# 368 instead of 384 columns in the dense U products of a PEER block: 16 inputs get their U vectors by gather during the gate build

## The chip, the cores and the metric

One core of one Trainium2 chip runs the whole program. The metric is the device time of one execution in microseconds (us); the kernel before takes 1673.26 us (median of 3 runs, 1672.77 to 1673.74). The engines are called as in the profile: PE (TensorE, matrix products), DVE (VectorE), ACT (ScalarE), POOL (GpSimd; it issues the indirect gathers), SP (SyncE; it issues most transfers).

## The reference, cut to what matters

The reference is one decoder layer for 512 inputs ("tokens") of width 1024. The change lies in its second half, a mixer of 16384 experts:

```
q = x @ w_query                                   # 8 heads, 2 halves of 128
s = q . sub_keys                                  # 128 scores for each half
16 best of each half -> 256 sums -> 16 best       # expert number e = i * 128 + j, gate g = softmax
act = gelu(u_table[e] . x)                        # 8 * 16 = 128 experts for each input
out = sum over the 128 experts of g * act * v_table[e]
```

The last lines of the layer are out_layer = layer_norm(ALPHA * x + out). Nothing is approximated in the kernel; float32 products are made of three products of split operands (high*high, high*low, low*high).

## The kernel before, in words

The 512 inputs are split in two. Inputs 384 to 511 (block 3) are served by **gathering**: for each of their 128 expert slots one row of u_table per input is fetched by an indirect DMA and multiplied on DVE, then the same with v_table (`gather`, L1259 on). Inputs 0 to 383 are served **densely**: all 16384 experts are computed for them, in 128 chunks of 128 experts. For chunk c, `u_chunk` (L1108) makes 8 * 3 = 24 products of 384 columns (L68 to L70, called from L1114) into one PSUM tile, and ACT writes the gelu of it to a tile "act" (L1116). Later `v_chunk` (L1249) multiplies that tile by the gates of the chunk (P, L1214), splits it into high and low parts (Ph L1227, Pl L1234) and makes 18 products of 512 columns with the chunk of v_table, which add to six PSUM tiles (`va`, L1243 to L1247). So a pair of one U chunk and one V chunk is 24 + 18 products.

The gates of the dense inputs must be there as a dense array: for every chunk of 128 experts and every input a gate or zero. `build_g` (L1025) makes it in 48 **groups** of 8 inputs. For a group, `hot` (L1028) compares the two halves of each expert number with an iota (two comparisons, oj L1036 and oi L1037) and multiplies one of the results by the high and low part of the gate (g L1038, oi L1039), all float16 on DVE; PE multiplies them (16 products of 128 columns, L1055 and L1056); ACT copies PSUM to a staging tile (L1058); after every fourth group SP stores that tile to DRAM (`gsp`, L1062). The V chunks read it back (`gt`, L1202): the first read needs all 12 stores, and the first P needs the first read.

Weights: every item (a chunk of u_table or v_table, 512 KB) goes through a stream: SP loads it to one of 3 raw tiles, ACT rounds it to the high part (wih, L105), DVE subtracts for the low part (wil, L115). The low part of item n + 2 is issued when item n is taken, and there are 3 tiles for it, so it waits until PE is done with item n - 1.

**The order of the work.** Each engine works strictly in program order, and the program is written by a planner at build time. Before the V chunks can start, 54 U chunks (LEAD, L1187) and the gates must be done. The planner (`drive`, L1154) keeps two sums: tm[0] is the time that it has given to PE (T_U = 4.24 for a U chunk, 1.1 for a group), tm[1] is that of DVE (2.7 for a group, 1.2 for the split of an item). Whenever tm[0] <= tm[1] and fewer than 54 U chunks have been written, it writes a U chunk, otherwise the next piece of DVE's work: routing (`stage1` L940, `stage2` L955), then the groups. What is left of the 54 U chunks is written after the last group (L1187). Then come the V chunks, each behind a U chunk until there are 128; the gather of block 3 is mixed into them at an even pace (L1338 to L1343).

The last part (`ln_out`, L1362) adds ALPHA * x to the sums, normalises and stores; for block 2 this is the end of the program.

Of the kernel before, what the change touches and what calls it, by code (L numbers as in the profile page):

```python
# [24 lines left out]
D = 1024  # L25
NB = 4
# [3 lines left out]
SCALE = 192.0 ** -0.5  # L30
NT = 384
LEAD = 54
LASTC = 120
T_U = 4.24
T_Q = 6.3
# [14 lines left out]
def tile_block(ctx: ExitStack, tc: tile.TileContext, I, out):  # L50
# [139 lines left out]
    gsp = dram.tile([NT // 32, 128, 128, 32], F32, name="gsp")  # L190
    acd = dram.tile([64, 128], F32, name="acd")

    wst = pool("wst")
# [662 lines left out]
    XTH = xt.tile([128, 8, S], F32R, name="XTH")  # L856
    XTL = xt.tile([128, 8, S], F32R, name="XTL")
    lnq = pool("lnq", side="right")
    ROW = lnq.tile([128, 2, D], F32, name="ROW")
# [95 lines left out]
    def stage2():  # L955
# [38 lines left out]
        sh = [128, 16, 16, 16]  # L994
        for b in range(NB):
            eq = rt2.tile([128, 16, 16, 16], F16, name="eq")
            abv = abf[:, b].rearrange("p e (h k) -> p (e h) k", k=16)
            V.tensor_tensor(eq, abv[:, :, None, :].to_broadcast(sh), iaE[:, None].to_broadcast(sh), op=OP.is_equal)
            yield 2.3
            eqv = eq.rearrange("p g a (k c) -> p (g a) k c", c=2)  # L1000
            tv = ti[:, b].rearrange("p e h a c -> p (e h a) c")
            V.tensor_tensor(eqv, eqv, tv[:, :, None, :].to_broadcast([128, 256, 8, 2]), op=OP.mult)
            yield 2.3
            for w in (8, 4, 2):
                V.tensor_tensor(eq[:, :, :w], eq[:, :, :w], eq[:, :, w:2 * w], op=OP.add)
# [5 lines left out]
    GT = {}  # L1011

    def g_head(b):
        ijg = IJG.pop(b)
        ps = px()
        for e in range(3):
            T.transpose(ps[:, e * 128:(e + 1) * 128], ijg[:, e].rearrange("p h k -> p (h k)"), ident)
        ijT = ijp.tile([128, 2, 128], F16, name="ijT", bufs=2)
        gT = ijp.tile([128, 2, 128], F16, name="gT", bufs=2)
        A.activation(ijT.rearrange("p a b -> p (a b)"), ps[:, 0:256], AF.Copy)  # L1020
        A.activation(gT[:, 0], ps[:, 256:384], AF.Copy, scale=GSC)
        V.scalar_tensor_tensor(gT[:, 1], ps[:, 256:384], GSC, gT[:, 0], op0=OP.mult, op1=OP.subtract)
        GT[b] = ijT, gT

    def build_g():  # L1025
        bc = [128, 4, 128, 2]

        def hot(n):  # L1028
            ijT, gT = GT[n // 16]
            t0 = n % 16 * 8  # L1030
            col = lambda z: z[:, t0:t0 + 8].rearrange("p (q c) -> p q c", c=2)[:, :, None, :].to_broadcast(bc)
            oj = gb.tile(bc, F16, name="oj", bufs=2)
            oi = gb.tile(bc, F16, name="oi", bufs=2)
            g1 = gb.tile(bc, F16, name="g1", bufs=2)
            io = iotaE[:, None].to_broadcast(bc)
            V.tensor_tensor(oj, io, col(ijT[:, 1]), op=OP.is_equal)  # L1036
            V.tensor_tensor(oi, io, col(ijT[:, 0]), op=OP.is_equal)  # L1037
            V.tensor_tensor(g1, oi, col(gT[:, 1]), op=OP.mult)  # L1038
            V.tensor_tensor(oi, oi, col(gT[:, 0]), op=OP.mult)  # L1039
            return oj, oi, g1  # L1040

        nxt = hot(0)
        yield 2.7
        for n in range(48):
# [18 lines left out]
            if g == 12 and b < 2:  # L1063
                g_head(b + 1)
            yield 2.7 if n < 47 else 0.1

# [37 lines left out]
    win.ha = 1  # L1104
    ap_ = pool("act")
# [71 lines left out]
    drive(fill)  # L1177
    close(rq)
    rt2 = pool("rt2")
    lo_on[0] = V  # L1180
    drive(stage2())
    close(rt2)
    close(rt)
    gb = pool("gb", side="right")
    drive(build_g())
    uc = un[0]
# [33 lines left out]
    def v_sb(c, nm):  # L1220
        if c > LASTC:
            return ap_.tile([128, NT], F32, name="act", bufs=LEAD).bitcast(F32R)
        return vst.tile([128, NT], F32R, name=nm, bufs=3)
# [138 lines left out]
    def ln_out(b):  # L1362
# [4 lines left out]
        for e in range(2):  # L1367
            V.scalar_tensor_tensor(t[:, ce[e]], t[:, ce[e]], ALPHA, va[b][e], op0=OP.mult, op1=OP.add)
            yield
# [13 lines left out]
        for e in range(2):  # L1383
# [102 lines left out]
```

## Time and profile before

| | |
|---|---|
| median of 3 runs | 1673.26 us |
| the profiled execution | 1676.3 us |
| its span, first to last instruction | 1674.3 us |
| PE / DVE / ACT / POOL busy | 97% / 81% / 41% / 27% |
| routing and gates, beside U chunks 2 to 53 | 540 to 829 us |
| first group of the gates / end of the last | 640 / 802.6 us |
| first V product | 829.3 us |
| last U chunk's gelu | 1439.9 us |

The profile shows one execution. Rows of a timeline give the start in us, the duration, the engine, the line of kernel.py, and the tiles (out<-in); in square brackets stands the idle time of the engine before it, and what ended that. In a table of windows each engine has its busy time and number of instructions (x), then the granted clock of TensorE (1.00 is full), the busy share of the DMA engines, and GB/s. "Busy" durations of neighbouring instructions on one engine overlap: the distance from one start to the next is what an instruction costs in a stream.

### The profile page before, as it was taken

The numbers are of one execution on the slowest core, as the hardware profiler recorded it, in microseconds if no ns is written. First come the engines' busy times: TensorE is split into PE (matmuls) and PEld (weight loads), VectorE is DVE, ScalarE is ACT, GpSimd is POOL, SyncE is SP. The second block draws the span as 40 slices with busy tenths as digits, with TensorE's granted clock in tenths as the row PEclk, the third lists the DMA queues.
The fourth block names the chain that finished last, engine by engine and source line by source line (L and its number), as shares of the span: only waits on it lengthen the run. The fifth ranks groups of instructions, "written<-read, shape, count | busy, mean of one in ns | idle before, by whom it ended". The sixth has DMA issues, their size and how long they took to land.

```text
span 1674.3 us, 23581 instructions
## 1 busy us (share of the span) xinstructions
PE 1622.4 (97%) x8639; PEld 1429.5 (85%) x8639; DVE 1363.2 (81%) x2674; ACT 685.0 (41%) x1082; POOL 450.6 (27%) x314
## 2 busy tenths in 40 slices
PE   7999989999999999999999999999999999999997
PEld 5877868888888998999999999999999999888886
DVE  8978688847399999999477878778788888989887
ACT  5573556631333344555433333333333333333331
POOL 0000000000333400000055555545454444653300
PEclk9999999999999999999999999999999999999999
DMA  6342121464432335667699999999999999999973
GB/s 238 102 151 76 45 62 46 111 237 138 124 96 76 101 114 158 244 227 258 203 361 341 330 322 332 330 346 319 321 339 335 333 321 341 341 351 332 339 228 124
DMA packets 146211, 384.80 MB, mean 230 GB/s; under 512 B 11936, under 2 KB 62368, under 8 KB 144304
## 3 DMA queue, kind: packets, MB, share of 16 engines
q1 hardware_dynamic: 105536, 237.24, 42.3%
q0 software_dynamic: 40416, 145.80, 24.3%
q8 instruction: 67, 1.10, 0.3%
q14 instruction: 48, 0.39, 0.1%
q10 hardware_dynamic: 144, 0.26, 0.0%
HBM read 350.72 MB, written 31.49 MB: 228 GB/s over the span
## 4 chain that ended last, share of the span: by engine, by line
PE 75%; DVE 20%; ACT 2%; issue 2%; DMA 1%; SPq 0%; DVEq 0%; ACTq 0%
PE va L1243 10%; PE va L1244 10%; PE va L1247 10%; PE pu L68 8%; PE pu L70 8%; PE pu L69 8%; DVE wil L115 2%; PE pa L69 2%; PE pa L70 2%; PE pa L68 2%; PE pw L69 1%; PE pw L70 1%; PE pw L68 1%; DVE t L931 1%; DVE g L1038 1%
## 5 line engine op out<-in xcount | busy, mean ns | idle before, releaser
L115 DVE TENSOR_TENSOR wil<-wir,wih 128x1024 fp32r<-128x1024 f32 (+1 forms) x250 | 297.4, 1190 | 113.0 <-issue 56.7
L105 ACT ACTIVATE wih<-wir 128x1024 fp32r<-128x1024 f32 (+2 forms) x269 | 277.9, 1034 | 228.5 <-DMA wir<-v 96.7
L70 PE MATMUL pu<-XTH,wil 128*128 128x384 f32 x1008 | 342.7, 340 | 4.7 <-DVE wil L115 4.7
L68 PE MATMUL pu<-XTH,wih 128*128 128x384 f32 x904 | 309.9, 343 | 1.0 <-ACT sc L917 1.0
L69 PE MATMUL pu<-XTL,wih 128*128 128x384 f32 x904 | 307.1, 340 | 0.0
L1280 POOL DMA_INDIRECT row<-u,ix x128 | 188.5, 1473 | 434.5 <-DMA wir<-v 262.1
L1244 PE MATMUL va<-wil,Ph 128*128 128x512 f32 x726 | 283.6, 391 | 0.0
L1280 POOL DMA_INDIRECT row<-v,ix x128 | 185.2, 1446 | 200.4 <-DVE ac L1297 170.8
L70 PEld LDWEIGHTS pu<-XTH,wil 128*128 128x128 f32 x1008 | 190.3, 189 | 5.0 <-DVE wil L115 5.0
L1116 ACT ACTIVATE act<-pu 128x384 f32<-128x384 f32 x126 | 61.9, 491 | 316.4 <-PE pu L70 316.3
L68 PEld LDWEIGHTS pu<-XTH,wih 128*128 128x128 f32 x904 | 170.9, 189 | 4.0 <-ACT sc L917 1.2
L69 PEld LDWEIGHTS pu<-XTL,wih 128*128 128x128 f32 x904 | 170.9, 189 | 2.8
L1243 PE MATMUL va<-wih,Ph 128*128 128x512 f32 x432 | 168.6, 390 | 0.0
L1297 DVE SCALAR_TENSOR_TENSOR ac<-row,hd,ac 128x1024 f32<-128x1024 f32 x128 | 164.0, 1281 | 2.5 <-DMA row<-v,ix 0.3
L1244 PEld LDWEIGHTS va<-wil,Ph 128*128 128x128 f32 x726 | 136.3, 188 | 26.2
L1291 DVE SCALAR_TENSOR_TENSOR row<-row,x 128x1024 f32<-128x1024 f32 x128 | 150.0, 1219 | 1.6 <-DMA row<-u,ix 1.5
L1247 PE MATMUL va<-wih,Pl 128*128 128x512 f32 x432 | 133.3, 390 | 0.0
L105 ACT ACTIVATE wihx<-wir 128x1024 fp32r<-128x1024 f32 x67 | 71.1, 1061 | 143.3 <-DMA wir<-v 88.3
L115 DVE TENSOR_TENSOR wil<-wir,wihx 128x1024 fp32r<-128x1024 f32 x61 | 74.6, 1223 | 63.0 <-issue 57.2
L1243 PE MATMUL va<-wihx,Ph 128*128 128x512 f32 x294 | 115.0, 391 | 1.2 <-ACT Ph L1227 1.2
L115 POOL TENSOR_TENSOR wil<-wir,wih 128x1024 fp32r<-128x1024 f32 x19 | 46.6, 2454 | 190.7 <-PE pw L70 164.2
L1247 PEld LDWEIGHTS va<-wih,Pl 128*128 128x128 f32 x432 | 81.2, 188 | 16.8
(435 smaller groups left out, 3067.7 us busy)
## 6 DMA issues: line engine op xcount, KB each, us to landing
wir<-ut SPq DMA_DIRECT2D x128, 512.0 KB, 5.2
wir<-v SPq DMA_DIRECT2D x128, 512.0 KB, 6.6
gsp<-stg SPq DMA_DIRECT2D x12, 2048.0 KB, 7.3
gt<-gsp SPq DMA_DIRECT2D x32, 768.0 KB, 10.0
wir<-wo SPq DMA_DIRECT2D x26, 512.0 KB, 4.1
wir<-wf SPq DMA_DIRECT2D x18, 512.0 KB, 3.5
wir<-wqr SPq DMA_DIRECT2D x16, 512.0 KB, 3.7
de<-acd POOLq DMA_DIRECT2D x8, 512.0 KB, 5.0
```

Source lines behind the costliest of these rows:

```text
L68: T.matmul(ps, lh, rh, start=start, stop=False)
L69: T.matmul(ps, lh, rl, start=False, stop=False)
L70: T.matmul(ps, ll, rh, start=False, stop=stop)
L105: A.activation(h, r, AF.Copy)
L115: self.lo(n).tensor_tensor(l, r, h, op=OP.subtract)
L1116: A.activation(ACT[c], ps, AF.Gelu)
L1243: T.matmul(va[b][e], Ph[:, bs], h[:, cs], start=c == 0, stop=False)
L1244: T.matmul(va[b][e], Ph[:, bs], l[:, cs], start=False, stop=False)
L1247: T.matmul(va[b][e], Pl[:, bs], h[:, cs], start=False, stop=c == 127)
L1280: G.indirect_dma_start(out=R[s], out_offset=None, in_=I["u"] if s < 128 else I["v"], in_offset=bass.IndirectOffsetOnAxis(ap=ix[:, s % 128: ...
L1291: V.scalar_tensor_tensor(r, r, 1.0, x3, op0=OP.mult, op1=OP.mult, accum_out=hd[:, s:s + 1])
L1297: V.scalar_tensor_tensor(ac, r, hd[:, s - 128:s - 127], ac, op0=OP.mult, op1=OP.add)
```

## The change

The dense U products take 368 columns (NU) instead of 384: the last UG = 16 inputs of block 2 leave them. For these 16 inputs the U vectors are gathered: 16 * 128 rows, taken as 16 indirect DMAs of 128 rows, each multiplied by x and summed on DVE (`ug_dots`), one after every second group from step 2 of the gate build on. Their gelu (128 partitions x 16) goes through DRAM into another layout and is multiplied into the gates of these inputs (`ug_head`, at step 41), scaled by its largest magnitude; the act tiles hold 1.0 in these 16 columns, and `ln_out` of block 2 multiplies the sum by the scale (and takes ALPHA * x from an ACT instruction). The routing treats block 2 first.

The rows and x for these products lie where 8 of the 54 act tiles were, so only 46 (KEEP) U chunks can be written before the last of the 16 products; the 8 others get a pool of their own after it (`act2`, step 34). The planner counts 4.07 for a U chunk, 2.55 for a group, and 1.2 for each gathered product. In `hot` the two comparisons become one instruction of twice the size.

```diff
 NT = 384
+UG = 16
+NU = NT - UG
 LEAD = 54
+KEEP = 46
-T_U = 4.24
+T_U = 4.07
...
-        for b in range(NB):
+        for b in (2, 0, 1, 3):
...
             if b == 2:
+                ug_index(p3)
+            if b == 1:
                 g_head(0)
...
+    def ug_index(tmp):
+        ijg = IJG[2]
+        f = lambda z: z.rearrange("p h k -> p (h k)")
+        ix = tmp[:, :128].bitcast(I32)
+        V.scalar_tensor_tensor(ix, f(ijg[:, 0]), 128.0, f(ijg[:, 1]), op0=OP.mult, op1=OP.add)
+        G.dma_start(ugi, ix[128 - UG:])
+        G.dma_start(ugg, f(ijg[128 - UG:, 2]))
+        G.dma_start(UR["ix"], bass.AP(tensor=ugi.tensor, offset=ugi.offset, ap=[[16, 8], [128, UG], [1, 16]]))
+        G.dma_start(UR["g"], ugg)
+        for n in range(2):
+            ug_fetch(n)
...
+    def ug_dots():
+        for n in range(16):
+            r = UR.pop(n)
+            V.scalar_tensor_tensor(r, r, 1.0, UR["x"], op0=OP.mult, op1=OP.mult, accum_out=UR["hd"][:, n:n + 1])
+            ug_fetch(n + 2)
+            yield 1.2
+        A.activation(UR["hd"], UR["hd"], AF.Gelu)
+        G.dma_start(bass.AP(tensor=ugh.tensor, offset=ugh.offset, ap=[[16, 8], [128, UG], [1, 16]]), UR["hd"])
+        G.dma_start(UR["w"], ugh)
+        close(ug)
+        aps.append(pool("act2"))
+        yield 0.1
+
+    def ug_head():
+        w, g = UR["w"], UR["g"]
+        mx, r = UR["m"][:, 0:1], UR["m"][:, 1:2]
+        V.tensor_tensor(w, w, g, op=OP.mult)
+        V.scalar_tensor_tensor(g, w, -1.0, w, op0=OP.mult, op1=OP.max)
+        V.tensor_reduce(mx, g, axis=AX.X, op=OP.max)
+        V.tensor_scalar(mx, mx, 1.0e-30, None, op0=OP.max)
+        V.reciprocal(r, mx)
+        V.tensor_scalar(w, w, r, None, op0=OP.mult)
+        G.dma_start(scl[128 - UG:], mx)
+        ps = px()
+        T.transpose(ps[:, :UG], w, ident[:UG, :UG])
+        gT = GT[2][1]
+        A.activation(gT[:, 0, 128 - UG:], ps[:, :UG], AF.Copy, scale=GSC)
+        V.scalar_tensor_tensor(gT[:, 1, 128 - UG:], ps[:, :UG], GSC, gT[:, 0, 128 - UG:],
+                               op0=OP.mult, op1=OP.subtract)
...
-            V.tensor_tensor(oj, io, col(ijT[:, 1]), op=OP.is_equal)
-            V.tensor_tensor(oi, io, col(ijT[:, 0]), op=OP.is_equal)
+            V.tensor_tensor(ij.rearrange("p e q i c -> p (e q) i c"), iotaE[:, None].to_broadcast(b2),
+                            ijT[:, n % 16].rearrange("p e (q c) -> p (e q) c", c=2)[:, :, None, :].to_broadcast(b2),
+                            op=OP.is_equal)
+            oi, oj = ij[:, 0], ij[:, 1]
...
-            yield 2.7 if n < 47 else 0.1
+            if n >= 2 and n % 2 == 0:
+                tm[1] += next(dots, 0.0)
+            if n == 41:
+                ug_head()
+                tm[1] += 1.2
+            yield 2.55 if n < 47 else 0.1
...
+    def act_tile():
+        k = an[0] % LEAD >= KEEP
+        an[0] += 1
+        return aps[k].tile([128, NT], F32, name="act", bufs=LEAD - KEEP if k else KEEP)
...
-        ps = (psum or pu)()[:, :NT]
+        ps = (psum or pu)()[:, :NU]
         for k in range(8):
-            mm3(ps, h[:, k], l[:, k], XTH[:, k, :NT], XTL[:, k, :NT], k == 0, k == 7)
-        ACT[c] = ap_.tile([128, NT], F32, name="act", bufs=LEAD)
-        A.activation(ACT[c], ps, AF.Gelu)
+            mm3(ps, h[:, k], l[:, k], XTH[:, k, :NU], XTL[:, k, :NU], k == 0, k == 7)
+        ACT[c] = act_tile()
+        A.activation(ACT[c][:, NU:], one, AF.Copy)
+        A.activation(ACT[c][:, :NU], ps, AF.Gelu)
...
-            if tm[0] <= tm[1] and un[0] < LEAD:
+            if tm[0] <= tm[1] and un[0] < (LEAD if len(aps) > 1 else KEEP):
...
+            if b == 2:
+                V.scalar_tensor_tensor(t[:, ce[e]], va[b][e], scl, t[:, ce[e]], op0=OP.mult, op1=OP.add)
+            else:
+                V.scalar_tensor_tensor(t[:, ce[e]], t[:, ce[e]], ALPHA, va[b][e], op0=OP.mult, op1=OP.add)
...
+    A.activation(xr[2], xr[2], AF.Copy, scale=ALPHA)
```

More of the change, by code (lines that the diff above doesn't have):

```diff
@@ L191, in tile_block @@
     acd = dram.tile([64, 128], F32, name="acd")
+    ugi = dram.tile([UG, 128], I32, name="ugi")
+    ugg = dram.tile([UG, 128], F32, name="ugg")
+    ugh = dram.tile([UG, 128], F32, name="ugh")
     wst = pool("wst")
@@ L857, in tile_block @@
     XTL = xt.tile([128, 8, S], F32R, name="XTL")
+    one = xt.tile([128, UG], F32, name="one")
+    scl = xt.tile([128, 1], F32, name="scl")
+    V.memset(one, 1.0)
+    V.memset(scl, 1.0)
     lnq = pool("lnq", side="right")
@@ L1178, in tile_block @@
     close(rq)
+    ug = pool("ug")
+    UR["x"] = ug.tile([128, D], F32, name="ux")
+    nc.sync.dma_start(UR["x"], bass.AP(tensor=xsp.tensor, offset=xsp.offset + (3 * 128 - UG) * D,
+                                       ap=[[0, 8], [D, UG], [1, D]]))
+    UR["ix"] = ijp.tile([128, 16], I32, name="uix")
+    UR["g"] = ijp.tile([UG, 128], F32, name="ugw")
     rt2 = pool("rt2")
@@ L1184, in tile_block @@
     gb = pool("gb", side="right")
+    UR["hd"] = gb.tile([128, 16], F32, name="uhd")
+    UR["w"] = gb.tile([UG, 128], F32, name="uw")
+    UR["m"] = gb.tile([UG, 2], F32, name="um")
     drive(build_g())
```

26 lines of the change are left out of this document (16 added, 10 removed).

## The prediction

> **What bounds the kernel now.** I read the table of windows first, cut at the borders of the stages: gate build, remaining U chunks, pairs of U and V chunks, V chunks alone, with one narrow window at the start of the pairs. "x" counts instructions; the last two numbers are DMA share and GB/s.
>
> ```profile
> 637.00:803.00 166.00, 157.81 (x1380) 150.48 (x1379) 155.64 (x221) 88.53 (x151) 0.00 (x0) 0.99 0.63 222
> 803.00:829.30 26.30, 25.08 (x143) 24.77 (x141) 5.48 (x6) 8.10 (x12) 0.00 (x0) 1.00 0.76 239
> 829.30:1440.00 610.70, 610.70 (x3068) 556.74 (x3069) 490.92 (x636) 216.49 (x296) 305.53 (x211) 1.00 0.94 330
> 850.00:900.00 50.00, 50.00 (x253) 45.60 (x252) 41.65 (x63) 17.70 (x24) 26.64 (x20) 1.00 0.99 358
> ```
>
> The columns are PE, PEld, DVE, ACT, POOL. From 829 on PE never pauses (610.70 of 610.70): it is the bound there, and a shorter product is a shorter stage. In the gate build it is otherwise: DVE works 155.64 of 166 us, PE 157.81. Both are full, so what is added to DVE there is paid. From 803 to 829 DVE is nearly idle (5.48 of 26.30) while PE works off U chunks. The gelus per stretch count them:
>
> ```profile
> 0.00:638.00 638.00, 14.37 (x26) 0.99 0.36 115
> 638.00:802.40 164.40, 12.28 (x25) 0.99 0.64 225
> 802.40:829.30 26.90, 2.46 (x5) 1.00 0.74 234
> ```
>
> The first count holds two table loads: 24 chunks before the first group, 25 beside the 48 groups, 5 after them. These 5 decide much of what follows, because the first V product must wait for a round trip of the last gates through DRAM. Here are its steps, from the timelines, the transfers and the chain that ended last:
>
> ```profile
> 802.39 0.22 PE L1056 MATMUL pw<-g,oj 128*128 128x128 f16 x1
> 803.30 0.33 SPq L1062 DMA_DIRECT2D gsp<-stg  x1
> gsp<-stg SPq DMA_DIRECT2D x12, 2048.0 KB, 7.3
> 821.71 6.35 DMA gt<-gsp
> 828.13 0.57 DVE P L1214
> 828.73 0.53 ACT Ph L1227
> 829.30 0.50 PE va L1243
> ```
>
> Store issued 0.9 after the last product, 7.3 to land, the read 6.35, P, Ph. Without a queue in between that is 0.9 + 7.3 + 6.4 + 0.1 + 0.6 + 0.6 = 15.9 us. Today it is hidden: 5 U chunks, and chunk 54 behind them, cover 26.9 us.
>
> **The change, part by part.**
>
> *The narrower product.* What counts is the distance of starts, not the duration:
>
> ```profile
> 1000.72 0.34 PE L68 MATMUL pu<-XTH,wih 128*128 128x384 f32 x1
> 1004.96 0.40 PE L1243 MATMUL va<-wih,Ph 128*128 128x512 f32 x1
> 1009.07 0.34 PE L68 MATMUL pu<-XTH,wih 128*128 128x384 f32 x1
> ...
> 217.75 0.28 PE L69 MATMUL pu<-wil,kvh 128*128 128x256 f32 x1
> 218.93 0.28 PE L70 MATMUL pu<-wih,kvl 128*128 128x256 f32 x1
> ```
>
> 24 products of 384 columns take 4.24 us, 0.177 each; the 18 of 512 take 4.11, 0.228 each; ten of 256 take 1.18, 0.118 each. So 16 columns are worth (0.228 - 0.177) / 8 = 6.4 ns by the upper neighbours and (0.177 - 0.118) / 8 = 7.3 ns by the lower; I take 6.9. A U chunk falls by 24 * 6.9 ns = 0.166 us, to 4.07. From V's start on there are 73 chunks on PE's path (55 to 127): **-12.1 us** (bounds -11.3 and -12.8). The stage can take it if the transfers can: they must rise from 330 to about 330 * 8.35 / 8.18 = 337 GB/s, and the narrow window shows 358 with PE at 50 of 50. The first two chunks, before 431 us, give -0.3.
>
> *What DVE gets in the gate build.* A group costs DVE the distance over its four instructions, a split that of L115, a gathered product that of L1291 with its read of the sum:
>
> ```profile
> 798.72 0.68 DVE L1036 TENSOR_TENSOR oj<-iotaE,ijT 128x1024 f16<-128x1024 f16 x1
> 799.32 0.68 DVE L1037 TENSOR_TENSOR oi<-iotaE,ijT 128x1024 f16<-128x1024 f16 x1
> 800.04 0.69 DVE L1038 TENSOR_TENSOR g<-oi,gT 128x1024 f16<-128x1024 f16 x1
> 800.77 0.69 DVE L1039 TENSOR_TENSOR oi<-oi,gT 128x1024 f16<-128x1024 f16 x1
> 801.38 1.22 DVE L115 TENSOR_TENSOR wil<-wir,wihx 128x1024 fp32r<-128x1024 f32 x1
> ...
> 1000.28 1.22 DVE L1291 SCALAR_TENSOR_TENSOR row<-row,x 128x1024 f32<-128x1024 f32 x1
> 1001.43 1.22 DVE L115 TENSOR_TENSOR wil<-wir,wih 128x1024 fp32r<-128x1024 f32 x1
> 1002.57 0.55 DVE L1234 TENSOR_TENSOR Pl<-P,Ph 128x384 fp32r<-128x384 f32 x1
> 834.12 0.28 DVE L1263 SCALAR_TENSOR_TENSOR ix<-ijg 128x128 int32<-128x128 f32 x1
> ```
>
> A group is 801.38 - 798.72 = 2.66 us, a gathered product 1.15, a split 1.14.
>
> - The merged comparison. One instruction of 2048 elements exists in the routing:
>
> ```profile
> L1005 DVE TENSOR_TENSOR eq<-eq 128x2048 f16<-128x2048 f16 x4 | 4.9, 1219 | 0.0
> L1036 DVE TENSOR_TENSOR oj<-iotaE,ijT 128x1024 f16<-128x1024 f16 x48 | 32.9, 686 | 5.0 <-PE pw L1056 4.9
> ```
>
> By durations it saves 2 * 686 - 1219 = 153 ns; by distances only one start, about 0.07 (1024 elements cost 0.60 from start to start, 2048 should cost 1.13). I take distances: 48 * 0.07 = **-3.4** (bounds -7.3 and 0).
> - 16 gathered products: 16 * 1.15 = **+18.4**. Their rows are asked for four groups ahead, over 10 us, so I cost POOL's part at nothing; if that cover fails, each costs a landing.
> - ug_head: seven small DVE instructions like L1263, at 0.28 or a little less, and a transpose and an ACT copy between the last two, on which DVE waits: **+2.4** (bounds 1 and 4). ug_index adds one (0.3); with T_U at 4.07 one more chunk is written before `stage2`, where POOL does the splits (one split less, -1.1): **-0.8** together.
> - Splits that move forward. With the new costs the planner writes U chunks faster: per group tm[1] gains 2.55 + 0.6 and tm[0] 1.1, a chunk closes 4.07 - 1.2 of the gap, so 0.71 chunks a group, where it is (2.7 - 1.1) / (4.24 - 1.2) = 0.53 today (48 groups: 25 chunks, as counted above). All 54 are then written before the last group, 5 more than today: 5 * 1.14 = **+5.7**.
> - The cap. At 0.71 a group the 46th chunk is written at group 28; the pool for the next comes at step 34. In between the gap grows by 6 * 2.05 = 12.3, so four chunks are then written in a row, before group 35's products. What that does to DVE is seen where U chunks run in a row today:
>
> ```profile
> 811.23 1.23 DVE L115 TENSOR_TENSOR wil<-wir,wih 128x1024 fp32r<-128x1024 f32 x1 [3.01 <-PE pu L70]
> 815.47 1.23 DVE L115 TENSOR_TENSOR wil<-wir,wih 128x1024 fp32r<-128x1024 f32 x1 [3.02 <-PE pu L70]
> ```
>
> Each split waits for a low tile until PE is done with an earlier chunk, and everything behind it on DVE, the next comparisons among it, waits too. Four in a row: three distances of 4.07 = 12.2, less 3.4 of splits, less what DVE was ahead, about **+8** (bounds 3 and 9). That is the wait that the change adds; PE is starved in turn from group 28 to 34 and again from 43 on.
>
> Sum: -3.4 + 18.4 + 2.4 - 0.8 + 5.7 + 8 = **+30.3** for the end of the last group, 802.4 -> 832.7. I laid the two engines' queues out instruction by instruction with these durations; for the kernel before this ends at 802.2, for the changed one at 832.7.
>
> *The round trip comes into the open.* No U chunk is left behind the last group but chunk 54 (4.07 us). First V product: 832.7 + 15.9 = 848.6 instead of 829.3, **+19.3** (bounds +7 and +27 from the terms above). PE stands idle some 12 us before it, and an idle PE starts slowly:
>
> ```profile
> 583.38 0.33 PE L69 MATMUL pu<-XTL,wih 128*128 128x384 f32 x1
> 588.43 0.69 PE L70 MATMUL pu<-XTH,wil 128*128 128x384 f32 x1 [4.72 <-DVE wil L115]
> 588.92 0.52 PE L68 MATMUL pu<-XTH,wih 128*128 128x384 f32 x1
> 593.08 0.38 PE L69 MATMUL pu<-XTL,wih 128*128 128x384 f32 x1
> ```
>
> After that pause 13 products take 0.32 apart instead of 0.177: 13 * 0.143 = **+2**.
>
> *At no cost:* the ACT copy of 16 ones per chunk (ACT 216 of 611 us beside the pairs; uncovered it would be a few tenths a chunk), the scaling of x for block 2 (ACT, while PE makes the last products; uncovered about 1 us), ln_out with another operand order (same shape), 8.4 MB of gathered rows in a stretch at 222 GB/s (about 50 more over 166 us, below the 358 shown).
>
> **Sum:** -0.3 + 19.3 + 2 - 12.1 = **+8.9 us**. The terms are of the profiled execution (1676.3 us, span 1674.3), 3.0 above the median of the runs; I add the difference to the median: 1673.26 + 8.9 = 1682.2, in a profiled execution about 1685.2.
>
> **The rivals.**
>
> - *DVE's work is hidden (faster).* If DVE could use its idle time of 803 to 829 before the last group, V's start would be bound by PE's work alone: 52 chunks * 0.166 = -8.6. Then -0.3 - 8.6 - 12.1 = -21, 1652 us. It decides from the point where the gates end before 829.3 - 8.6 - 15.9 = 805, that is at +2 instead of +30. Against it: DVE's 155.64 of 166. Halfway, faster by over 0.2% needs +18 at the gates' end. Chance 0.10.
> - *The catch-up does not stall, and the comparison saves its durations (no change).* 30.3 - 8 - 4 = +18.3 gives +7.3 at V's start, with the pause shorter +1: 7.3 + 1 - 12.4 = -4 to 0; without the one or the other about +1. Around 1672. Chance 0.15.
> - *The pairs do not get shorter (slower still).* Either transfers hold PE (share 0.94 today), or the weight load sets the distance of products. Then 19.3 + 2 = +21, 1694 us. Against it: 358 GB/s with PE full, and 0.118 us at 256 columns with a load for every product; the load is no floor at 0.17. Chance 0.07. By the Trainium skill ("TensorE: Matmul & The Clock Gate", Back-to-back issue gap) a stream of load-and-multiply pairs is spaced about 81 ns at 128 columns and 131 ns at 512, set by both; as an estimate 16 columns would then be worth 2 ns, a chunk 0.05 us, and the whole +17.5. This trace disagrees: 228 ns at 512 columns.
> - *The merged comparison falls to half the rate* through its other access pattern: 48 groups * 1 us more. Chance 0.01.
>
> The rest, 0.67, is the forecast.
>
> **How the numbers follow.** The likeliest is 1682.2. Its own range, from the bounds of its terms (V's start +9 to +26 within most of them, the pairs -11.3 to -12.8), is 1670 to 1690; the range of 8 in 10 reaches part of the way to the third rival and takes in most of the second: 1669 to 1692. A measurement of this kernel can tell about 0.2%, 3.3 us, from no change. Slower by more: most of the forecast and the third and fourth rivals, 0.74; within: 0.14; faster: 0.12.
>
> **What would show it.** In the profile after: U products 0.170 apart; no gelu between groups 29 and 34, then four within 17 us; a DVE wait of several us for PE before the fourth split of those; the last group near 833; the first V product about 16 us behind it, after a PE pause of over 10 us ended by DMA gt<-gsp; pairs of 8.18 us. I am wrong if gelus still stand behind the last group, or if the pairs stay at 8.35.

## The result: 1.0014 times the time before

After the change the kernel takes 1677.12 us (median of 20 runs, 1675.91 to 1678.37), beside 1674.45 us (20 runs) for the kernel before on the same chips: a ratio of **1.0014 [1.0008, 1.0020]**. That is 2.3 us slower by the ratio, where 8.9 us were forecast. The profiled executions say the same: spans of 1676.0 and 1674.3 us, +1.7.

The windows of the kernel after, cut where its stages end (PE, PEld, DVE, ACT, POOL, then granted clock, DMA share, GB/s):

```profile
637.00:833.00 196.00, 172.98 (x1470) 165.55 (x1470) 176.04 (x216) 97.53 (x189) 25.20 (x17) 0.95 0.66 239
833.00:847.00 14.00, 5.73 (x29) 5.42 (x26) 0.56 (x1) 1.27 (x3) 0.00 (x0) 0.74 0.74 253
847.00:1442.00 595.00, 594.87 (x3067) 540.76 (x3068) 491.21 (x635) 223.36 (x371) 304.46 (x211) 0.99 0.95 339
```

The gate build is longer, and neither engine is full in it any more: DVE works 176 of 196 us, PE 173. Then come 14 us with PE at 5.73, the round trip of the last gates, now in the open. From 847 on PE is full again, with the transfers at 339 GB/s.

The gelus (L1191) in four stretches; the first holds two table loads:

```profile
0.00:639.00 639.00, 14.42 (x27) 0.99 0.36 118
639.00:757.00 118.00, 9.56 (x20) 1.00 0.75 275
757.00:778.00 21.00, 0.48 (x1) 0.76 0.47 180
778.00:833.20 55.20, 3.82 (x8) 0.90 0.54 191
```

These are 25 chunks before the first group and 29 beside the groups, all 54 ahead of the last group's end, and a hole from 757 to 778 with one chunk in it, where PE's clock is granted at 0.76.

The round trip, from the queue of SP, the chain that ended last, and the timelines of DVE and PE:

```profile
834.11 0.33 SPq L1125 DMA_DIRECT2D gsp<-stg  x1
840.58 1.18 SPq L1286 DMA_DIRECT2D gt<-gsp  x2
840.58 5.16 DMA gt<-gsp
845.96 0.56 DVE L1298 TENSOR_TENSOR P<-act,gt 128x384 f32<-128x384 f32 x1 [14.46 <-DMA gt<-gsp]
838.40 0.33 PE L73 MATMUL pu<-XTH,wil 128*128 128x368 f32 x1
847.13 0.79 PE L1327 MATMUL va<-wihx,Ph 128*128 128x512 f32 x1 [8.40 <-ACT Ph L1311]
```

The store is issued at 834.11, the first read, which needs it, 6.5 us later at 840.58; the read takes 5.16, P begins at 845.96, the first V product at 847.13. The last product of chunk 54 begins at 838.40, so PE has stood idle for 8.4 us by then.

And the distance of products in the pairs:

```profile
1202.69 0.33 PE L71 MATMUL pu<-XTH,wih 128*128 128x368 f32 x1
1206.69 0.39 PE L1327 MATMUL va<-wihx,Ph 128*128 128x512 f32 x1
1210.80 0.33 PE L71 MATMUL pu<-XTH,wih 128*128 128x368 f32 x1
```

A U chunk now takes 4.00 us, 166.7 ns a product; 4.07 was forecast from 4.24.

Against the prediction, profiled execution to profiled execution:

| | before | after | difference | predicted |
|---|---|---|---|---|
| first group's first product | 640.4 | 639.8 | -0.7 | (one sum) |
| last group's products end | 802.4 | 833.1 | +30.7 | +30.3 |
| first V product | 829.3 | 847.13 | +17.8 | +19.3 - 0.3 |
| first V product to gelu of chunk 55, counted from 0 (cold PE) | 8.7 | 11.2 | +2.5 | +2 |
| 72 pairs | 8.360 each | 8.107 each | **-18.2** | **-12.1** |
| V chunks alone | | | -0.7 | 0 |
| tail | | | +0.3 | 0 |
| sum | | | +1.7 | +8.9 |

The working of the gate build and the round trip came out within 1.5 us. Nearly all of the miss is in one row: the narrower product saves half as much again as I gave it.

### The profile page after: what moved, and what is told of

Read it like the earlier page. It is cut to its first block, busy times and chain, and to the rows that moved or that the text cites. A ratio compares the mean times of both kernels' runs of the same rounds, so it can differ in the third digit from the quotient of the medians.

```text
span 1676.0 us, 23763 instructions
## 1 busy us (share of the span) xinstructions
PE 1598.8 (95%) x8640; PEld 1407.4 (84%) x8640; DVE 1378.2 (82%) x2667; ACT 698.7 (42%) x1213; POOL 478.6 (29%) x338
## 4 chain that ended last, share of the span: by engine, by line
PE 73%; DVE 22%; ACT 2%; issue 2%; DMA 1%; DVEq 0%; ACTq 0%; SPq 0%
PE va L1327 10%; PE va L1331 10%; PE va L1328 10%; PE pu L71 8%; PE pu L73 8%; PE pu L72 8%; PE pa L72 2%; PE pa L73 2%; PE pa L71 2%; DVE wil L118 2%; DVE ij L1096 2%; PE pw L72 1%; PE pw L73 1%; PE pw L71 1%; DVE t L941 1%
## 5 line engine op out<-in xcount | busy, mean ns | idle before, releaser
L73 PE MATMUL pu<-XTH,wil 128*128 128x368 f32 x1008 | 334.2, 332 | 4.8 <-DVE wil L118 4.6
L71 PE MATMUL pu<-XTH,wih 128*128 128x368 f32 x904 | 301.3, 333 | 1.0 <-ACT sc L927 1.0
L72 PE MATMUL pu<-XTL,wih 128*128 128x368 f32 x904 | 299.1, 331 | 0.0
L1191 ACT ACTIVATE act<-pu 128x368 f32<-128x368 f32 x126 | 60.0, 476 | 241.0 <-PE pu L73 240.8
L118 POOL TENSOR_TENSOR wil<-wir,wih 128x1024 fp32r<-128x1024 f32 x20 | 48.4, 2421 | 193.4 <-PE pw L73 167.1
## 6 DMA issues: line engine op xcount, KB each, us to landing
gt<-gsp SPq DMA_DIRECT2D x32, 768.0 KB, 10.1
```

The lines of the kernel that those rows point to most:

```text
L71: T.matmul(ps, lh, rh, start=start, stop=False)
L72: T.matmul(ps, lh, rl, start=False, stop=False)
L73: T.matmul(ps, ll, rh, start=False, stop=stop)
L118: self.lo(n).tensor_tensor(l, r, h, op=OP.subtract)
L1191: A.activation(ACT[c][:, :NU], ps, AF.Gelu)
```

## The experiments

### What a product of a given width costs

My 6.9 ns for 16 columns came from the distances at 256, 384 and 512 columns. The first question was whether the line between them is straight. **e1_widths** leaves out the whole layer: bare chains of products at 20 widths, three products of split operands with a weight load each, no transfers beside them.

> This kernel computes nothing of the reference: it runs chains of 24 products (8 weights, high*high, high*low, low*high, a weight load before each, as in a U chunk) at widths of 256 to 512 columns, three chains for each width, with no transfers beside them; then 368 columns from column 16 on, 384 from column 128 on, and 384 and 368 on operands whose rows are 384 instead of 512 long. The question is why 16 columns were worth 10.1 ns in the changed kernel (spacing 0.1767 us at 384, 0.1666 at 368) and not the 6.9 that I had taken between 256, 384 and 512 columns. Theory A: the spacing is no straight line in the width, it has a step of some 3 ns between 368 and 384. Then 384 shows 0.1767 here too, 368 shows 0.1666, 376 or 380 lies on one of the two sides with a jump, and elsewhere 16 columns cost 6.4 to 6.9 ns. Theory B: the products' spacing is a straight line (0.43 ns a column) and the changed kernel gained the rest from something beside the products (transfers, ACT, DVE). Then 384 and 368 differ by 6.9 ns here, and the level of one of them differs from its kernel. Theory C: it is the place of the operand (where a row ends in memory), then 368 from column 16 and the rows of 384 differ from the others.

First products of chains of 72 of 368, 372, 376, 380, 384 and 388 columns; the distance between two starts is 72 products:

```profile
130.89 0.33 PE L83 MATMUL pu<-XH,WH 128*128 128x368 f32 x1
142.90 0.33 PE L83 MATMUL pu<-XH,WH 128*128 128x372 f32 x1
155.13 0.34 PE L83 MATMUL pu<-XH,WH 128*128 128x376 f32 x1
167.61 0.34 PE L83 MATMUL pu<-XH,WH 128*128 128x380 f32 x1
179.93 0.34 PE L83 MATMUL pu<-XH,WH 128*128 128x384 f32 x1
192.42 0.34 PE L83 MATMUL pu<-XH,WH 128*128 128x388 f32 x1
```

368: 12.01 / 72 = 166.8 ns; 384: 12.49 / 72 = 173.5. With N for the number of columns, 10 of the 20 widths lie within 1 ns of N / 2.4 + 13.3 ns (256: 119.9, 320: 146.7, 512: 227.3, measured); the other ten are 1.2 to 6.5 ns off it (448: 206.5). From 368 to 384, 16 columns cost 6.7 ns here, close to the 6.9 that I had taken, and 368 comes out as in the kernel. It is 384 that differs: 173.4 here, 176.7 in the kernel before. The step between 368 and 384 (A) fell, and so did the two places that C had named: 368 from column 16 on and rows of 384 gave 166.7 and 173.4 again. What B said of this run came true; that the rest came from beside the products it could not show. What was left was that the kernel before ran 3.3 ns above this level for a reason of its own.

**e2_narrow_only** is the kernel before with 368 columns and nothing else; the 16 inputs get 1.0 in place of their gelu.

```diff
-            mm3(ps, h[:, k], l[:, k], XTH[:, k, :NT], XTL[:, k, :NT], k == 0, k == 7)
+            mm3(ps, h[:, k], l[:, k], XTH[:, k, :NU], XTL[:, k, :NU], k == 0, k == 7)
-        A.activation(ACT[c], ps, AF.Gelu)
+        A.activation(ACT[c][:, NU:], one, AF.Copy)
+        A.activation(ACT[c][:, :NU], ps, AF.Gelu)
```

> The kernel before with the U products at 368 columns and nothing else of the change: no gather, two comparisons, the old planner costs and the old pool; the 16 inputs that leave the dense products get 1.0 in place of their gelu, so their part of the output is left out. Theory A (the narrower product itself is worth 0.24 to 0.25 us a chunk): pairs of 8.10 us, 73 chunks save 18, the first V product comes about 1 us earlier, the first two chunks give 0.6; total -20, ratio 0.988, 1654 to 1655 us. By the size that the prediction used (0.166 a chunk): -12.1 - 1 - 0.3 = -13.4, ratio 0.992. Theory B (the gain came from elsewhere in the change): pairs of 8.19 or more.

Measured: 0.9897 [0.9882, 0.9913] (1659.75 beside 1676.66), pairs of 8.133 us (so B fell), 166.9 ns a product, first V product at 830.21. So this kernel gains 17 us without the rest of the change (its operand lies at another place too, see below); the size forecast (0.992) lies outside the interval. The first V product moved by +0.9, not -1. The gelu of the third chunk is already 3.8 us late (544.8 beside 541.0): at 430 us PE waits 2.96 us for XTL, where the kernel before waits 0.33 (the kernel after waits 2.95). From that gelu to the first V product e2 is 2.9 us shorter.

### Where the 3.3 ns come from

**f1_modes** asks again with bare chains (the layer left out): after chains of other widths, alternating with 18 products of 512, with other tiles, with the same weights for all products, beside transfers, beside work of DVE and ACT.

> Computes nothing of the reference. The first sweep gave 0.1733 us at 384 columns, where the kernel before runs 0.1767 in all its U chunks, and 0.1667 at 368 in both: so a straight N / 2.4 + 13.3 ns for both widths in the sweep, and 3.4 ns more for 384 inside the kernel. This one runs 384 and 368 columns after chains of other widths, alternating with 18 products of 512 columns as in the V chunks, with other places of the moving operand, with one weight for all products, beside 12 transfers of 512 KB, and beside DVE and ACT work. Theory A2 (384 has two regimes, 416 and 424 cycles a product, and what ran before decides which): some of the sequences show 0.1767 for 384 columns, and 368 stays at 0.1667 in all. Theory B2 (other traffic on the chip costs the 3.4 ns): only the stretches with transfers or with DVE and ACT show 0.1767. Theory C2 (the place of the operands): only the stretches with other operands do. If none does, the cause stays open.

384 columns took 173.3 to 174.5 ns everywhere (174.4 to 174.5 where they alternate with 512), 368 took 166.5 to 166.9. None showed 176.7, so nothing that was tried here raises 384 columns to what the kernel has. For C2 that settles little: by the build's addresses its other tiles lay only 64 bytes off the weights' place modulo 256 (next runs).

**g1_380, g2_376, g3_372, g4_352** are e2 with `UG` set to 4, 8, 12 and 32, one run each. The gelus of so many inputs are 1.0.

> The kernel before with U products of 380 columns and nothing else of the change (4 inputs get 1.0 in place of their gelu, their output is left out). What is a column worth inside this kernel? By the sweep (theory A3: the spacing of a width is the same everywhere except for 384, which is slow here): 0.1712 us, pairs of 8.23, that is over half of what 368 columns gave. By a straight line between this kernel's 384 and 368 (theory B3): 0.1742, pairs of 8.30. By the prediction's 0.43 ns a column: 0.1750.

> As before with 376 columns, 8 inputs left out. Sweep (A3): 0.1733. Straight line (B3): 0.1717. The prediction's size: 0.1733. Pairs of 8.28, 8.24, 8.28.

> As before with 372 columns, 12 inputs left out. Sweep (A3): 0.1700. Straight line (B3): 0.1692. The prediction's size: 0.1715. Pairs of 8.20, 8.18, 8.24.

> As before with 352 columns, 32 inputs left out. Sweep (A3): 0.1600 to 0.1610, 6 to 7 ns below 368, as 16 columns at 2.4 a nanosecond. Straight line through 384 and 368 (B3): 0.1567. The prediction's size: 0.1629 below its own 0.1767, or 0.1598 below 368. Pairs of 7.96 or 7.88.

Measured: 1665.76, 1663.84, 1659.16 and 1647.59 us beside 1676.62; 173.2, 170.5, 167.1 and 160.2 ns a product. 380 is dear, 372 nearly as cheap as 368. Neither the widths of e1 nor a straight line give these four numbers. So something changed from kernel to kernel that I hadn't meant to change. The build's addresses show it: XTH and XTL, the operand that PE streams, share a pool with the small tile `one`, whose size goes with `UG`, and start lower by what is added to that pool. The rounded weights lie at 128 modulo 256 bytes in all of these kernels; XTH lies at 224 in the kernel before, at 160 in e2 and g3, at 192 in g1 and g2, at 96 in g4, at 128 in the bare chains, and at **128 in the kernel after**, where the new tiles `one` (64 bytes) and `scl` (32 bytes) moved it by 96.

**h1_places** (bare chains of 384 and 368, the layer left out) moves the operands to 17 sets of places.

> Computes nothing of the reference. Chains of 384 and 368 columns as in the first sweep, on operands in 17 placements within one large tile: weights low and moving operand high as in the kernel, the two exchanged, both moving parts shifted by 64 to 2048 bytes, one of them shifted against the other, the weights shifted by 64 to 2048 bytes, and weights rotating through three tiles. Theory C4 (where the operands lie against each other in SBUF sets the extra nanoseconds, so 384 costs 0.1767 in the kernel and 0.1733 in the sweep): the spacing at 384 varies between placements by 3 ns or more, and some show 0.1767. Rival (placement does not matter): 0.1733 and 0.1667 in all of them, within 1 ns; then what raises 384 in the kernel stays open.

Multiples of 256 bytes changed nothing (173.3 and 166.7). The moving operand 128 bytes further: 176.0 and 173.2. Only the low part of it 64 bytes further: 173.8 and 169.6; the weights 64 bytes further: 174.6 and 168.8, which is what a shift of the moving operand by 192 gives in the next run (174.7 and 168.9). So the place of one read operand against the other, modulo 256 bytes, matters, by up to 6.5 ns a product.

**i3_shifts** (the same bare chains) shifts the moving operand against the weights in steps of 32 bytes.

> Computes nothing of the reference. Chains of 384 and 368 columns with the moving operand shifted against the weights by 0 to 256 bytes in steps of 32, and of 380, 376, 372 and 352 columns by 0 to 160 bytes. Theory C5: at 384 columns 0.1733 at 0, 64 and 256 bytes and 0.1767 at 96 (the kernel before); at 368 0.1667 at 0 and 32; at 380 and 376 and 64 bytes 0.1733 and 0.1706, at 372 and 32 bytes 0.1676, as the kernels of these widths had them. If the shift of a kernel gives another value here than in the kernel, something beside the place counts.

First products of chains of 72: 384 columns at shifts of 0 and 32 bytes, then at 96 and 128; 368 columns at 0 and 32, then at 96 and 128:

```profile
59.48 0.33 PE L73 MATMUL pu<-Z 128*128 128x384 f32 x1
71.99 0.34 PE L73 MATMUL pu<-Z 128*128 128x384 f32 x1
...
96.95 0.34 PE L73 MATMUL pu<-Z 128*128 128x384 f32 x1
109.67 0.34 PE L73 MATMUL pu<-Z 128*128 128x384 f32 x1
...
172.41 0.33 PE L73 MATMUL pu<-Z 128*128 128x368 f32 x1
184.40 0.33 PE L73 MATMUL pu<-Z 128*128 128x368 f32 x1
...
208.49 0.33 PE L73 MATMUL pu<-Z 128*128 128x368 f32 x1
220.96 0.33 PE L73 MATMUL pu<-Z 128*128 128x368 f32 x1
```

At 384 columns: 12.51 / 72 = 173.7 ns without a shift (173.3 within the chain), 12.72 / 72 = 176.7 with 96 bytes. At 368: 166.6 without, 173.2 with 96. A table of the values within the chains against the kernels:

| kernel | columns, shift | in the table | in the kernel |
|---|---|---|---|
| before | 384, 96 | 176.7 | 176.7 |
| g1 | 380, 64 | 173.3 | 173.2 |
| g2 | 376, 64 | 170.5 | 170.5 |
| g3 | 372, 32 | 166.7 | 167.1 |
| e2 | 368, 32 | 167.7 | 166.9 |
| g4 | 352, 224 | 160.0 (at 160) | 160.2 |
| after | 368, 0 | 166.7 | 166.6 |
| i1 (below) | 384, 0 | 173.3 | 174.5 |
| i2 (below) | 368, 96 | 173.3 | 169.0 |

(352 columns were measured at shifts up to 160 only, where they took 160.0 to 166.7, so g4 tests nothing.) Of the eight others six agree within 1 ns. i1 is 1.2 above the table, and 173.3 in its chunks ahead of the groups, where no V products stand between them; f1 showed much the same for chains that alternate with 512 (174.4). i2 takes the table's 173.3 in one stretch (its chunks from 601 to 630 us) and 168.7 to 169.0 in others (549 to 590, and the pairs).

The table also says that 16 columns have no single price: from 384 to 368 they are worth 6.7 ns without a shift and 3.4 at 96 bytes.

**i1_before_pad96** is the kernel before with an unused tile of 96 bytes in the pool of XTH, which then lies at 128:

```diff
+    pad = xt.tile([128, 24], F32, name="pad")
+    V.memset(pad, 1.0)
```

> The kernel before, unchanged in all its work, with 96 bytes of an unused tile behind the moving operand of the U products, so that XTH and XTL lie 96 bytes lower: at 128 modulo 256, as the weights do, and as in the changed kernel (where the tiles of ones and of the scale stand behind them). In the kernel before they lie at 224 modulo 256. The sweep of placements showed up to 6.5 ns a product by shifts below 256 bytes. Theory C5 (the changed kernel's 10.0 ns for 16 columns are 16 / 2.4 = 6.7 for the columns and 3.4 for the place): the spacing at 384 falls from 0.1767 to 0.1733, a U chunk by 0.08 us, pairs from 8.36 to 8.28, 73 chunks by 6 us, the first two by 0.2; ratio 0.996 to 0.9965. Rival (the place has no part in it inside the kernel): 0.1767 and no change.

Measured: **0.997** [0.9959, 0.9981] (1671.22 beside 1675.89); its span is 1668.2.

```profile
1197.34 0.33 PE L68 MATMUL pu<-XTH,wih 128*128 128x384 f32 x1
1201.53 0.39 PE L1245 MATMUL va<-wih,Ph 128*128 128x512 f32 x1
1205.65 0.33 PE L68 MATMUL pu<-XTH,wih 128*128 128x384 f32 x1
```

4.19 us a U chunk (174.5 ns a product) instead of 4.24, pairs of 8.307 on the mean, where 8.28 were expected. 96 unused bytes are worth some 5 us.

**i2_after_xo** is the opposite: the kernel after with `one` and `scl` in a pool of their own elsewhere, so that XTH lies at 224 again.

```diff
-    one = xt.tile([128, UG], F32, name="one")
-    scl = xt.tile([128, 1], F32, name="scl")
+    xo = pool("xo", side="right")
+    one = xo.tile([128, UG], F32, name="one")
+    scl = xo.tile([128, 1], F32, name="scl")
```

> The changed kernel with its two small tiles (ones and scale) in a pool of their own, so that XTH and XTL lie at 224 modulo 256 again, as in the kernel before; nothing else changes. Theory C5: the spacing at 368 rises from 0.1667 to about 0.170 (the columns alone: 0.1767 - 0.0067), pairs from 8.11 to 8.19, the time by 5 to 7 us; ratio to the kernel before about 1.0045 to 1.0055, near the +8.9 us of the prediction (1.0053). Rival: 0.1667 and 1.0014 as the changed kernel.

Measured: **1.0051** [1.0037, 1.0065] (1684.77 beside 1675.89).

```profile
1201.84 0.33 PE L71 MATMUL pu<-XTH,wih 128*128 128x368 f32 x1
1205.90 0.39 PE L1328 MATMUL va<-wih,Ph 128*128 128x512 f32 x1
1209.98 0.33 PE L71 MATMUL pu<-XTH,wih 128*128 128x368 f32 x1
```

A U chunk takes 4.06 here. So of the 10.1 ns a product that the change saved, 7.7 are the columns and 2.4 the place (by i1, in the other order, 7.9 and 2.2). With the place taken back the change costs 8.9 us, the number forecast, but the agreement is in part chance: the first V product is at 853.05 (+23.7 instead of +19) and the pairs bring -16.3 instead of -12.1. In whole pairs the place is worth less than in the U products: 8.133 here beside 8.107 in the kernel after, where 8.19 were expected, because the V products are shorter here (4.08 us instead of 4.11). That is 1.9 us over 72 pairs; i1 has 3.8.

Most of what separates the two kernels lies ahead of the pairs: the groups begin 4.0 us later than in the kernel after and take 2.0 longer. Of the 4.0, 3.5 are there before a third U chunk is done (its gelu is at 545.4 beside 541.9). What runs in between is the query projection, 16 times 24 products of 512 columns that stream the same operand. First products of two neighbouring runs of 24 in i2, then in the kernel after:

```profile
460.88 0.48 PE L71 MATMUL pw<-XTH,wih 128*128 128x512 f32 x1
467.37 0.48 PE L71 MATMUL pw<-XTH,wihx 128*128 128x512 f32 x1
...
459.13 0.48 PE L71 MATMUL pw<-XTH,wih 128*128 128x512 f32 x1
465.48 0.48 PE L71 MATMUL pw<-XTH,wihx 128*128 128x512 f32 x1
```

6.49 us beside 6.35 (233.2 and 227.1 ns a product); the kernel before has 6.49 too, and i1 6.35. Sixteen times 0.14 are 2.2 us. Beside that the granted clock is lower in i2 from 430 to 445 us, 0.77 instead of 0.89; that this makes the other 1.3 is not shown.

### What the gate build costs

First the three steps that could be read from the trace of the kernel after. A group's four instructions on DVE, up to the split behind them:

```profile
747.93 1.22 DVE L1096 TENSOR_TENSOR ij<-iotaE,ijT 128x2048 f16<-128x2048 f16 x1
749.18 0.69 DVE L1100 TENSOR_TENSOR g<-ij,gT 128x1024 f16<-128x1024 f16 x1
749.91 0.69 DVE L1101 TENSOR_TENSOR ij<-ij,gT 128x1024 f16<-128x1024 f16 x1
750.52 1.22 DVE L118 TENSOR_TENSOR wil<-wir,wih 128x1024 fp32r<-128x1024 f32 x1
```

2.59 us instead of 2.66: the merged comparison saves one start, as forecast, and not 0.15. The gathered products, from the costliest groups, with the idle time before them last:

```profile
L1046 DVE SCALAR_TENSOR_TENSOR urow<-urow,ux 128x1024 f32<-128x1024 f32 x16 | 19.5, 1218 | 0.0
```

No idle time ahead of any of the 16: POOL's gathers are hidden. The four chunks in a row, on DVE:

```profile
775.75 1.22 DVE L118 TENSOR_TENSOR wil<-wir,wih 128x1024 fp32r<-128x1024 f32 x1
780.67 1.23 DVE L118 TENSOR_TENSOR wil<-wir,wih 128x1024 fp32r<-128x1024 f32 x1 [3.70 <-issue]
784.67 1.23 DVE L118 TENSOR_TENSOR wil<-wir,wih 128x1024 fp32r<-128x1024 f32 x1 [2.77 <-PE pu L73]
788.67 1.23 DVE L118 TENSOR_TENSOR wil<-wir,wihx 128x1024 fp32r<-128x1024 f32 x1 [2.77 <-PE pu L73]
789.81 1.22 DVE L1096 TENSOR_TENSOR ij<-iotaE,ijT 128x2048 f16<-128x2048 f16 x1
```

They come as forecast: from 775.75 to 789.81 DVE does four splits and stands idle for 9.24 us, of which the profile puts 5.54 down to PE. Whether these waits cost the end of the groups as much as I said (+8) is another matter.

**e4_nodots** takes the price of the gathered products away. Each product is replaced by a copy of one column; the gathers, the planner's costs and the order stay.

```diff
-            V.scalar_tensor_tensor(r, r, 1.0, UR["x"], op0=OP.mult, op1=OP.mult, accum_out=UR["hd"][:, n:n + 1])
+            V.tensor_copy(UR["hd"][:, n:n + 1], r[:, 0:1])
```

> The changed kernel without the 16 gathered products on DVE: each is replaced by a copy of one column (about 0.1 us), so the 16 inputs get wrong activations; the rows are still fetched, the planner writes the same order. It asks what the 18.4 us of added DVE work cost in place. If DVE's sum alone set the end of the gate build (a straight addition, as in the prediction's sum), the last group ends 16 to 18 us earlier, near 816, and the time falls by as much, ratio 0.991. Laid out as queues, PE and DVE wait for each other (the cap, the four chunks in a row, the last groups without U chunks stay), and PE's own work takes over as the bound: the last group ends only 5 to 7 us earlier, near 827, ratio 0.997 to 0.998.

Measured: 0.9973 [0.9964, 0.9982] (1671.81); the last group ends at 826.9. Some 17 us less of DVE's work move that end by only 6.2. A sum that adds each removed instruction falls; the two queues laid out instruction by instruction hold.

**f3_spread** takes the run of four apart: after the pool for the last 8 tiles opens, at most one U chunk between two of DVE's pieces.

```diff
-            if tm[0] <= tm[1] and un[0] < (LEAD if len(aps) > 1 else KEEP):
+            if tm[0] <= tm[1] and un[0] < (LEAD if len(aps) > 1 else KEEP) and not (last[0] and un[0] > KEEP):
```

> The changed kernel, its cap of 46 U chunks kept, but after the cap at most one U chunk is written between two pieces of DVE's work, so the four in a row behind step 34 become one per group. The prediction put +8 us on the wait behind the four: if that wait is a loss of its own, the last group ends at 825 and the time falls by 8, ratio to the kernel before 0.9965. Laid out as queues, the wait only moves: PE has stood without U chunks from group 28 to 34 and has the same eight to make, so the last group ends about 831.5 instead of 833, ratio 1.000 to 1.001.

Measured: 0.9985 [0.9975, 0.9994] (1673.33); the last group ends at 830.4, 2.7 earlier: between the two, nearer the second. So the catch-up did not cost 8 us in the end; most of its wait is one that comes without it too.

**e3_tu44** changes one constant of the kernel after: the planner counts 4.4 for a U chunk, so that it writes fewer of them between the groups.

```diff
-T_U = 4.07
+T_U = 4.4
```

> The changed kernel with one constant of the planner changed: a U chunk is counted at 4.4 us of PE instead of 4.07, so that chunks are written later. Laid out by hand, the 46th chunk is then written after step 34 (no stop at the cap, no four in a row), and 3 chunks are left behind the last group. My theory (what the change loses is the stall behind the four chunks, the splits moved ahead, and the round trip of the last gates without cover): the last group ends near 820 instead of 833, the first V product comes at 836 to 838 instead of 847, without a pause of PE of over 4 us and without slow products after it; total 11 to 13 us less than the changed kernel, about 1665, ratio to the kernel before 0.994 to 0.995. Rival (DVE is the bound of that stage by the sum of its work alone, so the order matters little): the first V product within 2 us of 847, ratio 1.001.

Measured: **0.9953** [0.9940, 0.9967] (1667.74; span 1665.2). The last group ends at 820.3, three chunks are left behind it, there is no long pause, and the first V product is at 839.08, a little later than expected. It is faster than the kernel before and the kernel after; of the whole change only its variant f2 below is as fast. Its round trip, on SP's queue and DVE:

```profile
821.18 0.33 SPq L1125 DMA_DIRECT2D gsp<-stg  x1
829.90 0.33 SPq L90 DMA_DIRECT2D wir<-ut  x1
830.45 2.83 SPq L1286 DMA_DIRECT2D gt<-gsp  x2
837.87 0.56 DVE L1298 TENSOR_TENSOR P<-act,gt 128x384 f32<-128x384 f32 x1 [8.00 <-DMA gt<-gsp]
```

The window of that stretch:

```profile
820.40:839.00 18.60, 16.16 (x98) 15.85 (x96) 3.08 (x4) 5.94 (x12) 0.00 (x0) 1.00 0.86 283
```

16.7 us from the store to P, where the kernel after takes 11.9: PE is busy for 16.16 of 18.60 with the U chunks left, the transfers run at 283 GB/s instead of 253, and the first read stands behind a weight load on SP's queue. **f2_tu44_gtpool** asks whether that queue costs anything: the first two reads go over POOL's.

```diff
-            nc.sync.dma_start(gt[q], gsp[:, :, q * 4:(q + 1) * 4, :].rearrange("b j i t -> j b i t"))
+            (G if q < 2 else nc.sync).dma_start(gt[q], gsp[:, :, q * 4:(q + 1) * 4, :].rearrange("b j i t -> j b i t"))
```

> The kernel with the U chunk counted at 4.4, and the first two reads of the gates (gt) issued on POOL's queue instead of SP's. In that kernel the first V product came 18.8 us after the last group, against 14.0 in the changed kernel: SP issues the read only behind the loads for the 3 U chunks that are left, which wait for raw tiles. Theory: with POOL the read goes out as soon as the last store has landed, the first V product comes right behind PE's last U chunk, at 836.5 instead of 839.1, total 2 to 3 us less, 0.9935 to 0.994 of the kernel before. Rival (the landing of the store itself is what is late): no change, 0.9953.

```profile
822.16 0.33 SPq L1125 DMA_DIRECT2D gsp<-stg  x1
...
830.65 2.10 POOL L1286 DMA_DIRECT2D gt<-gsp  x2 [29.75 <-DMA wir<-ut]
```

Measured: 0.9951 [0.9937, 0.9964] (1667.33), first V product at 840.01: no gain. The read goes out 8.5 us after the store's issue instead of 9.3, but P begins 16.6 us after it instead of 16.7. So SP's queue costs nothing. That the store's landing is what is late is not shown by itself: the profile puts POOL's wait down to the landing of the weight load that was issued 0.4 us behind the store.

## Why the prediction was right or wrong, point by point

- **The step that failed is the price of the narrower product:** "So 16 columns are worth (0.228 - 0.177) / 8 = 6.4 ns by the upper neighbours and (0.177 - 0.118) / 8 = 7.3 ns by the lower; I take 6.9." They were worth 10.1 ns. What it misses is that the row of 384 columns, the one to be changed, holds some nanoseconds that belong to the place of its operand and not to its width: 3.4 in the bare chains (176.7 at 96 bytes, 173.3 without a shift), 2.2 in the pairs of i1. The change moved that operand by 96 bytes. -12.1 became -18.2. Of the 6.1 us between them the U products make 72 * 24 * 2.3 ns = 4.0 by the place and 72 * 24 * 0.9 ns = 1.6 by the columns (7.7 to 7.9 ns instead of 6.9). In whole pairs the place is 1.9 (i2) to 3.8 us (i1), so how the 6.1 divide is known only to some 2 us. The bounds that I gave (-11.3 and -12.8) came from the same three rows, so they could not hold it. I read a table of widths as if width were all that differed between its rows.
- **The gate build's end** came where the sum put it (+30.3, measured +30.7), but not by its terms, which cannot be added. The +18.4 for the gathered products is worth 6.2 at the end when they are taken out (e4), the +8 for the catch-up 2.7 (f3); and with the operand at the old place, where a U chunk of the pairs takes 4.06, close to the 4.07 that I had reckoned with, the end is at 839.1 (i2), 36.7 later than before and not 30.3. As a sum the agreement is in good part luck. Single durations were right: 2.59 a group, 1.15 a gathered product, no wait for the gathers; ug_head takes 2.2 instead of 2.4. The layout of both queues was the better tool: for e4 it gave the right end where the plain addition was 11 off.
- **The planner's order** held: 54 chunks before the last group, a hole without gelus, then four in a row (780.6, 784.6, 788.6, 792.6). One chunk more than forecast stands ahead of the first group.
- **The round trip came into the open** as forecast, and took 14.0 us, not 15.9: the read went out 6.5 after the store's issue, where I had put 7.3 for the landing, and took 5.16 instead of 6.35, with PE idle for most of it. Here a round trip priced from a stretch with U chunks in it was too dear for one without.
- **The cold start** cost 2.5 where 2 was given: the granted clock is 0.50 from 842.9 to 853.0 us, that is for 5.9 us from the first V product on, and 1.00 from 853.1 to 860. By the Trainium skill ("TensorE: Matmul & The Clock Gate", Part 1: The HAM clock gate) PE falls to half its clock when it has been idle and needs some us of work to get it back. The trace agrees.
- **The rivals.** "DVE's work is hidden" fell: the gates end 31 us later. "The pairs do not get shorter" fell. The Trainium skill's 131 ns at 512 columns ("TensorE: Matmul & The Clock Gate", Back-to-back issue gap) disagree with the chain of e1 too, which took 227.3. The half-rate comparison fell: 1.22 us. The second rival, no change, came nearest in time (around 1672), but not by its mechanism: it had V's start at +7.3, and that came at +17.8; of its two reasons the comparison's durations fell, and the catch-up was in part right: by f3 it cost 2.7, not 8.

The change as a whole is a trade of 17.8 us ahead of the first V product and 2.5 in the cold start against 18.2 in the pairs. e3 shows that the first side was not fixed: one constant of the planner gives 8 us of it back (first V product at 839.08 instead of 847.13).

What stays open: why certain shifts cost; why i2's 368 columns at 96 bytes take 173.3 ns, as in the bare chain, in one stretch and 169.0 in the pairs, and its V products 4.08 us instead of 4.11; and why the columns are worth 7.7 to 7.9 ns in the pairs where the bare chains have 6.7 or 3.4.

## What to carry to other kernels

Before a price per column, per row or per byte is read from neighbours in a trace, one asks what else differs between these rows; a short measurement of the operation by itself at the very size in question shows whether the row that is to be changed stands where its size puts it. An edit that adds a small tile moves the tiles behind it, and that alone can be worth as much as the edit. Where two engines wait for each other in turn, added work is laid out in both queues: here 17 us of work on the busier one were 6 us at the end.

## What the runs showed of the hardware that was not expected

- In bare chains a product with a weight load of its own took 119.9, 146.7, 173.4 and 227.3 ns at 256, 320, 384 and 512 columns, within 1 ns of N / 2.4 + 13.3. Between them it is no straight line: 372 took 170.0, 376 173.4, 380 171.2, and 448 took 206.5, 6.5 above.
- The place of the streamed operand against the weights, modulo 256 bytes, changed that by up to 6.6 ns: 384 columns 176.7 at 96 bytes, 176.0 at 128, 174.7 at 192 and 173.3 at 0, 32, 64, 160, 224 and 256; 368 columns 173.3 at 96 and 128 and 166.7 to 168.9 elsewhere. In the whole kernels 512 columns of the query projection took 233.2 at 96 bytes and 227.1 without a shift. What in the chip does this no run shows.
- In the stretch with one U chunk in 21 us the granted clock fell to 0.76 on the mean: it is 0.50 from 767.8 to 777.9.
